# Placing norm, key and value pieces among the steps of the mixers, and the early banks of the merges, in a one-core hybrid decoder layer

## The chip, the core and the metric

The kernel runs on one core of a Trainium2 chip. A core has five engines with queues of their own: TensorE (PE in the profile: matmuls, with weight loads as PEld), VectorE (DVE), ScalarE (ACT), GpSimd (POOL) and SyncE (SP), the last of which only issues transfers here. The metric is the device time of one execution in microseconds; lower is better. The time before is 2633.38 us, the median of three runs (2632.34 to 2636.46).

## What is computed

One layer with 512 tokens of width 2048, in float32. The input is normalised and modulated to u, and one combined projection of u feeds three causal mixers in parallel:

```python
proj = jnp.einsum('bsd,de->bse', u, w_in)
o_a = diff_attention(a_q, a_k, a_v, lam, lam_init, da_norm_w)   # 8 heads, q and k in two maps of 64, v 128
o_b = retention(b_q, b_k, b_v, ret_norm_w)                      # 8 heads, rotated qk of 64, v 128
o_c = dilated_mixture(c_q, c_k, c_v)                            # 3 groups x 8 heads
y_a = jnp.einsum('bsw,wd->bsd', o_a * jax.nn.silu(a_z), w_proj_a)   # y_b and y_c likewise
merged = jax.nn.sigmoid(g_a) * y_a + jax.nn.sigmoid(g_b) * y_b + jax.nn.sigmoid(g_c) * y_c
y = jnp.einsum('bsd,de->bse', merged, w_out)
return x + gate[:, None] * y                                    # then one final RMSNorm
```

The outputs of differential attention and of retention are normalised per head (an RMS norm over the 128 channels of a head) and multiplied by silu of a gate column. That norm, the queries and keys of these two mixers, and the banks of the merges are what the change places anew.

## The kernel before

Every product is made of three matmuls, since each operand is held as a rounded high part and a low remainder: `mm3` issues high by high, high by low, low by high. Splitting an operand costs one ScalarE copy (the high part) and one VectorE subtraction (the low part), so behind each weight tile that TensorE reads stand one ACT `wh` and one DVE `wl`.

Behind the modulation (from L702) the instructions of the engines are pinned (L72), but for some transfers of POOL: each engine runs them in the order in which the program issues them. The order is thus written by hand, and an instruction that waits holds up all behind it on its engine.

**The step (L747).** The mixers and merges are cut into steps. `step()` issues the load of a later weight tile on SP (`feed`), the split of the tile that the second step from here will use (`cut`: `wh`, then `wl`), then every piece that lies in the list `late`, and hands out the tile that was split two steps ago. The caller then issues 24 matmuls with it (`half_mul`, L808: half of a projection of 128 columns). So the pieces of a step run on ACT and DVE beside the 24 matmuls of that step, and behind `wh` and `wl` of it. Weight tiles have three buffers each (`wr`, `wh`, `wl`).

**Banks.** The eight accumulator banks are two with the tag `pj` (projections) and six with the tag `at` (all else). A new tile takes a bank of its tag whose readers are done, and the matmul that writes it waits for them.

**Differential attention (L1367 to L1450)** takes one head at a time, in six steps `run(0)` to `run(5)`: queries' projection (0, 1), keys' (2, 3), gate column's (4, 5), then the scores of eight tiles (`a_scores`: each a DVE instruction `e<-at,cau` that adds the mask, and an exponential). `a_rest` is the list of what is left of a head, done in the six steps of the next one, as (piece within the step, piece after its matmuls): silu of the gate column; then the transposes; then the values; the squares for the norm, then their sum on PE; `gate`, which is `rms_gate` (ACT square root, DVE reciprocal of 128x512, two products); `put` (`yh`, `yl`, the split of the result for the merge). Beside them the loop places `query` in step 2, `keys` in step 4, two pieces `part` that sum a modulation row (steps 1 and 2), `values_split` (even heads, step 4) and, in heads 3 and 7, `gate_split` (step 5). `keys` makes four copies and two subtractions on a half of the partitions each, then two copies more.

**Retention (L1515 to L1591)** takes two heads at a time in eight steps: queries (0, 1), keys (2, 3), gate column of the first head (4, 5), scores of the first head, gate column of the second head (6), scores of the second head, (7), values of the first head. These four projections take turns on the two `pj` banks, so that the gate column of step 4 needs the bank of the queries and that of step 6 the bank of the keys. `rotate` reads a projection from its bank with four ACT copies (`rt`) and a DVE product (`rf<-pj,cos`). `query` runs in step 3, `keys` in step 4. `b_rest` has three entries, done in steps 0 to 2 of the next pair: silu and the squares of the first head, then on PE their sum and the values of the second head; squares of the second head, the whole norm of the first with its `put`, then a sum; the whole norm of the second head with its `put`.

**The merges (`gate_phase`, L832)** multiply the mixer's result by its output weights, 16 tiles of columns, each summed into a bank. The first six (four for the last merge, `AHEAD`, L767) begin before the mixer's last y tiles are there: `y_start` does the rows that exist, and the pieces `left` of the last head or pair are placed among these steps; `close` adds the missing rows and reads the bank with a DVE product. `close` of tiles 0 and 1 follows the seventh `y_start`, of 2 and 3 the eighth. Tiles 0 and 1 take `pj` banks, all others `at` banks (L841). Merge "first" follows the dilated windows, "mid" the attention, "last" the retention.

## Time and profile before

| stretch of the profiled execution | us | PE busy us | DVE busy us | ACT busy us | granted clock |
|---|---|---|---|---|---|
| first merge, 1611 to 1715 us | 104.0 | 102.5 | 41.7 | 36.2 | 1.00 |
| differential attention, 1715 to 2031 | 316.0 | 306.0 | 230.0 | 185.7 | 0.99 |
| mid merge, 2031 to 2128.5 | 97.5 | 92.5 | 55.2 | 29.4 | 0.98 |
| retention, 2128.5 to 2351 | 222.5 | 206.7 | 148.7 | 124.9 | 0.95 |
| last merge, 2351 to 2448 | 97.0 | 90.7 | 63.9 | 32.1 | 0.96 |
| whole span | 2634.7 | 2537.7 | 1924.4 | 1132.7 | 0.987 |

The profiled execution took 2636.43 us, 3.05 more than the median of the three timed runs, with 2634.7 us from its first to its last instruction. The busy times come from the profile's windows of each stretch, the last row from its page. A matmul of 512 columns is shown 0.39 us long, but the next one starts 0.23 us after it, since they are pipelined. The granted clock is the mean share of TensorE's full clock.

### The profile page before, as it was taken

The page shows a single profiled execution, that of the slowest core. Times are in us where ns is not written, and L with a number is a line of the kernel's source. Part 1 is how long each engine was busy: PE and PEld are TensorE (multiplying, and loading weights), DVE is VectorE, ACT ScalarE, POOL GpSimd, SP SyncE. Part 2 cuts the span into 40 slices and gives each one's busy share as a digit, 9 for nine tenths or more (in the row PEclk, how much of TensorE's full clock was granted, in tenths as well). Part 3 has the DMA queues.
Part 4 walks back from the last instruction along what each step waited for, and adds up shares of the span by engine and source line. Part 5 has one row for each costly group of instructions (what it writes and reads, how often), then busy time and mean ns, then how long its engine had stood idle before and what let it go on. Part 6 is the DMA issues. An engine that isn't in the chain of part 4 may idle for free. (4 is left out here: it accounts for less than half of the span.)

```text
span 2634.7 us, 36774 instructions
## 1 busy us (share of the span) xinstructions
PE 2537.7 (96%) x14539; PEld 2234.8 (85%) x14539; DVE 1924.4 (73%) x2682; ACT 1132.7 (43%) x1476; POOL 262.2 (10%) x327
## 2 busy tenths in 40 slices
PE   6999999999999999999999999999998999989998
PEld 5777877999999999998888888887787887777888
DVE  7994888778887787878786775367777557676654
ACT  4223433433443333333346665346656245553223
POOL 2342000000000000000000001200000210003200
PEclk9999999999999999999999999999999999999999
DMA  9776766666766666666665554653342663338643
GB/s 343 257 273 221 270 212 208 216 208 208 233 229 224 219 220 223 231 226 227 223 203 159 154 153 136 205 151 108 109 120 73 211 191 98 99 109 255 209 134 117
DMA packets 363953, 504.83 MB, mean 192 GB/s; under 512 B 18850, under 2 KB 237748, under 8 KB 363396
## 3 DMA queue, kind: packets, MB, share of 16 engines
q1 hardware_dynamic: 329732, 401.89, 47.7%
q0 software_dynamic: 27136, 92.13, 10.3%
q10 hardware_dynamic: 6912, 8.46, 0.9%
q8 instruction: 114, 1.87, 0.3%
q14 instruction: 59, 0.48, 0.1%
HBM read 450.37 MB, written 52.04 MB: 191 GB/s over the span
## 5 line engine op out<-in xcount | busy, mean ns | idle before, releaser
L86 ACT CAST xh<-xr 128x2048 fp32r<-128x2048 f32 x196 | 374.1, 1909 | 590.8 <-PE at L86 470.6
L86 DVE TENSOR_TENSOR xl<-xr,xh 128x2048 fp32r<-128x2048 f32 x196 | 449.1, 2291 | 187.3 <-ACT xh L86 186.2
L86 PE MATMUL pj<-uh,wh 128*128 128x512 f32 x944 | 376.2, 399 | 15.8 <-DVE rf L86 15.8
L86 DVE TENSOR_TENSOR wl<-wr,wh 128x1024 fp32r<-128x1024 f32 (+2 forms) x241 | 238.1, 1007 | 205.1 <-ACT wh L86 200.0
L86 PE MATMUL pj<-uh,wl 128*128 128x512 f32 x944 | 372.0, 394 | 2.6 <-POOL wl L172 2.6
L86 PE MATMUL pj<-ul,wh 128*128 128x512 f32 x944 | 372.1, 394 | 0.0
L86 ACT CAST wh<-wr 128x1024 fp32r<-128x1024 f32 (+2 forms) x275 | 239.1, 889 | 294.8 <-PE at L86 158.4
L86 DVE TENSOR_TENSOR xr<-xr 128x512 f32<-128x512 f32 x448 | 309.2, 690 | 16.0 <-DMA xr<-in_w_in_dram 4.6
L86 PE MATMUL at<-fh,xl 128*128 128x256 f32 x864 | 244.9, 283 | 2.1 <-DVE xl L86 2.1
L86 PE MATMUL at<-fh,xh 128*128 128x256 f32 x864 | 244.5, 283 | 0.0
L86 PE MATMUL at<-fl,xh 128*128 128x256 f32 x864 | 244.4, 283 | 0.0
L86 PEld LDWEIGHTS pj<-uh,wh 128*128 128x128 f32 x944 | 180.3, 191 | 53.2 <-DVE rf L86 17.0
L86 PEld LDWEIGHTS pj<-uh,wl 128*128 128x128 f32 x944 | 179.6, 190 | 41.6 <-POOL wl L172 3.0
L86 PEld LDWEIGHTS pj<-ul,wh 128*128 128x128 f32 x944 | 180.3, 191 | 36.3
L86 PEld LDWEIGHTS at<-fh,xl 128*128 128x128 f32 x864 | 165.8, 192 | 2.5 <-DVE xl L86 2.5
L86 PEld LDWEIGHTS at<-fh,xh 128*128 128x128 f32 x864 | 165.8, 192 | 0.0
L86 PEld LDWEIGHTS at<-fl,xh 128*128 128x128 f32 x864 | 165.8, 192 | 0.0
L86 PE MATMUL at<-uh,xh 128*128 128x256 f32 x576 | 163.0, 283 | 0.0
L86 PE MATMUL at<-ul,xh 128*128 128x256 f32 x576 | 163.0, 283 | 0.0
L86 PE MATMUL at<-uh,xl 128*128 128x256 f32 x576 | 163.0, 283 | 0.0
L86 PE MATMUL at<-yh,wh 128*128 128x512 f32 x336 | 132.2, 394 | 9.3 <-ACT wh L86 6.2
L86 PE MATMUL at<-yh,wl 128*128 128x512 f32 x336 | 131.7, 392 | 0.0
(387 smaller groups left out, 5702.2 us busy)
## 6 DMA issues: line engine op xcount, KB each, us to landing
xr<-in_w_in_dram SPq DMA_DIRECT2D x224, 512.0 KB, 4.6
xr<-in_w_in_dram SPq DMA_DIRECT2D x84, 1024.0 KB, 5.0
wr<-in_w_in_dram SPq DMA_DIRECT2D x116, 512.0 KB, 4.0
wa<-in_w_ada_dram SPq DMA_DIRECT2D x20, 1024.0 KB, 9.5
wr<-in_w_out_dram SPq DMA_DIRECT2D x32, 512.0 KB, 3.9
wr<-in_w_in_dram SPq DMA_DIRECT2D x32, 448.0 KB, 8.7
wb<-in_w_ada_dram SPq DMA_DIRECT2D x12, 1024.0 KB
bw<-in_w_in_dram SPq DMA_DIRECT2D x24, 384.0 KB, 5.5
```

The source lines that it names most:

```text
L86: return lambda *a, **k: pin(f(*a, **k))
```

## The change

Four things are moved; no arithmetic is added or taken away.

1. `rms_gate` is cut in two: `rms_root` (the square root on ACT) and `rms_gate` (reciprocal and two products on DVE).
2. Attention: in step 4 the order is square root, `keys`, then the rest of the norm; `keys` makes its last four copies in another order. The two `part` pieces go one step later (2 and 3), and `values_split` goes from step 4 of an even head to step 1 of the odd head behind it.
3. Retention: `query` goes from step 3 to step 2; in each step the pair's own piece goes ahead of what is left of the pair before. What is left is spread over steps 0 to 4: the first head's norm in step 1, its `put` in step 2, the second head's norm in step 3, its `put` in step 4. In the last pair the values of the first head go ahead of step 7, its squares into step 7, and the values of the second head ahead of the last merge.
4. Merges: tile 0, the last early tile (5, or 3 in the last merge) and tiles 10 and 15 take the `pj` banks, all others `at`.

```diff
@@ -838,7 +838,7 @@
 
         def y_start(db, nj):
             h, l = step()
-            py = pj() if db < 2 else at()
+            py = pj() if db in (0, n_ahead - 1, 10, 15) else at()
             for j in range(nj):
                 mm3(py, h[:, j, :], l[:, j, :], yh[j], yl[j], j == 0, j == 7)
             ahead[db] = py
@@ -861,8 +861,8 @@
 
         for db in range(n_ahead):
             before, after = left.pop(0) if left else (None, None)
-            if before is not None:
-                late.append(before)
+            if before:
+                late.extend(before if isinstance(before, tuple) else (before,))
             y_start(db, 8 - lacking)
             if after is not None:
                 after()
@@ -1241,13 +1241,15 @@
         dve.tensor_sub(sqs[64:P, :], sq[0], sqs[0:64, :].bitcast(F32))
         return sqs
 
-    def rms_gate(pool, o, ps, wcol, sz):
+    def rms_root(pool, ps):
         rs = pool.tile([P, S], F32, tag="rs", name="rs", bufs=1)
         act.activation(out=rs, in_=ps, func=AF.Sqrt, scale=1.0 / P, bias=eps)
+        return rs
+
+    def rms_gate(rs, o, wcol, sz):
         dve.reciprocal(rs, rs)
         dve.scalar_tensor_tensor(out=rs, in0=o, scalar=wcol, in1=rs, op0=ALU.mult, op1=ALU.mult)
         dve.tensor_mul(rs, rs, sz)
-        return rs
 
     a_es, ap = open_pool("ap", "left")
     cau = ap.tile([P, 512], F32, tag="cau", name="cau")
@@ -1383,13 +1385,16 @@
         def total():
             got["ps"] = rms_sum(got["sqs"])
 
+        def root():
+            got["rs"] = rms_root(ap, got["ps"])
+
         def gate():
-            got["y"] = rms_gate(ap, got["o"], got["ps"], daw, got["sz"])
+            rms_gate(got["rs"], got["o"], daw, got["sz"])
 
         def put():
-            put_y(ap, hd, got["y"])
-
-        return [(first, None), (None, turn), (None, values), (squares, total), (gate, None), (put, None)]
+            put_y(ap, hd, got["rs"])
+
+        return [((first,), None), ((), turn), ((), values), ((squares,), total), ((root, gate), None), ((put,), None)]
 
     def query(ps, qs):
         for m in range(2):
@@ -1408,16 +1413,17 @@
             dve.tensor_sub(kl[own, :], ps[own, :], kh[own, :].bitcast(F32))
         for (kh, kl), (own, other) in zip(ks_, sides):
             act.copy(kh[other, :], kh[own, :].bitcast(F32))
+        for (kh, kl), (own, other) in zip(ks_, sides):
             act.copy(kl[other, :], kl[own, :].bitcast(F32))
 
-    rest, chunk = [(None, None)] * 6, {}
+    rest, chunk = [((), None)] * 6, {}
     gate_load(0)
     gate_load(1)
     for hd in range(8):
         def run(i, ps, *pieces):
 
             before, after = rest[i]
-            late.extend(f for f in (before,) + pieces if f is not None)
+            late.extend(before[:1] + tuple(f for f in pieces if f is not None) + before[1:])
             half_mul(ps, i % 2, step())
             if after is not None:
                 after()
@@ -1431,16 +1437,16 @@
         n, last_part = hd // 4, hd % 4 == 3
         ps = pj()
         run(0, ps)
-        run(1, ps, lambda: part(0))
+        run(1, ps, (lambda: values_split(*v)) if hd % 2 else None)
         qs = [ap.tile([P, S], F32R, tag=f"q{m}", name=f"q{m}") for m in range(2)]
         qps, ps = ps, pj()
-        run(2, ps, lambda: query(qps, qs), lambda: part(1))
+        run(2, ps, lambda: query(qps, qs), lambda: part(0))
         if hd % 2 == 0:
             v = values_of(ap, 0, hd * P)
-        run(3, ps)
+        run(3, ps, lambda: part(1))
         ks_ = [tuple(ap.tile([P, S], F32R, tag=f"k{m}{x}", name=f"k{m}{x}") for x in "hl") for m in range(2)]
         kps, ps = ps, pj()
-        run(4, ps, lambda: keys(kps, ks_), (lambda: values_split(*v)) if hd % 2 == 0 else None)
+        run(4, ps, lambda: keys(kps, ks_))
         run(5, ps, (lambda: chunk.update(parts=gate_split(n))) if last_part else None)
         es, sts = [], []
         a_scores(qs, ks_, es, sts)
@@ -1513,32 +1519,44 @@
 
 
     def b_rest(pr, ps, got, values):
-        def first():
-            got["sz"].append(silu(bp, ps, tag="sz1", bufs=1))
-            got["sqs"] = rms_squares(bp, got[0], "0")
-
-        def total():
-            got["ps"] = rms_sum(got["sqs"])
-
-        def second():
-            total()
+        def squares(a):
+            got["s", a] = rms_squares(bp, got[a], str(a))
+
+        def total(a):
+            got["p", a] = rms_sum(got["s", a])
+
+        def root(a):
+            got["r", a] = rms_root(bp, got["p", a])
+
+        def gate(a):
+            rms_gate(got["r", a], got[a], ret_col, got["z", a])
+
+        def put(a):
+            put_y(bp, 2 * pr + a, got["r", a])
+
+        def z():
+            got["z", 1] = silu(bp, ps, tag="sz1", bufs=1)
+
+        def value():
             got[1] = values(1)
 
-        def between():
-            sqs = rms_squares(bp, got[1], "1")
-            put_y(bp, 2 * pr, rms_gate(bp, got[0], got["ps"], ret_col, got["sz"][0]))
-            got["sqs"] = sqs
-
-        def last():
-            put_y(bp, 2 * pr + 1, rms_gate(bp, got[1], got["ps"], ret_col, got["sz"][1]))
-
-        return [(first, second), (between, total), (last, None)]
-
-    rest = [(None, None)] * 3
+        def both(*fs):
+            return lambda: [f() for f in fs]
+
+        if pr < 3:
+            return [((z, lambda: squares(0)), both(lambda: total(0), value)),
+                    ((lambda: squares(1), lambda: root(0), lambda: gate(0)), lambda: total(1)),
+                    ((lambda: put(0),), None), ((lambda: root(1), lambda: gate(1)), None),
+                    ((lambda: put(1),), None)]
+        return [both(lambda: squares(0)), both(value, lambda: total(0)),
+                (both(z, lambda: squares(1), lambda: root(0), lambda: gate(0)), lambda: total(1)),
+                (both(lambda: put(0), lambda: root(1), lambda: gate(1)), None), (lambda: put(1), None)]
+
+    rest = [((), None)] * 5
     for pr in range(4):
         def run(i, ps, *pieces):
-            before, after = rest[i] if i < 3 else (None, None)
-            late.extend(f for f in (before,) + pieces if f is not None)
+            before, after = rest[i] if i < 5 else ((), None)
+            late.extend(pieces + before)
             half_mul(ps, i % 2, step())
             if after is not None:
                 after()
@@ -1571,24 +1589,30 @@
         run(1, qps)
         decs = [decay(2 * pr + a) for a in range(2)]
         kps = pj()
-        run(2, kps)
+        run(2, kps, lambda: query(qps))
         v = values_of(bp, 1, 2 * pr * P)
-        run(3, kps, lambda: query(qps))
+        run(3, kps)
         zps = pj()
         run(4, zps, lambda: keys(kps))
         run(5, zps, lambda: values_split(*v))
-        pts, got = ([], []), {"sz": []}
+        pts, got = ([], []), {}
         b_scores(2 * pr, ks_[0], qs[0], pts[0], decs[0])
         ps = pj()
-        run(6, ps, lambda: got["sz"].append(silu(bp, zps, tag="sz0", bufs=1)))
+        run(6, ps, lambda: got.update({("z", 0): silu(bp, zps, tag="sz0", bufs=1)}))
         b_scores(2 * pr + 1, ks_[1], qs[1], pts[1], decs[1])
-        run(7, ps)
 
         def values(a, pr=pr, v=v, pts=pts):
             return b_values(2 * pr + a, *v, pts[a])
 
-        got[0] = values(0)
         rest = b_rest(pr, ps, got, values)
+        if pr < 3:
+            run(7, ps)
+            got[0] = values(0)
+        else:
+            got[0] = values(0)
+            run(7, ps, rest[0])
+            rest[1]()
+            rest = rest[2:]
     m_es, mh, ml = None, [], []
 
     def merged_open():
```

## The prediction

> **What bounds the kernel now.** First the page, for the engine that is the bound; then the waits of that engine over the whole span, of which these belong to the stages that the change touches; then the windows of the stretches at half clock behind them.

> ```profile
> PE 2537.7 (96%) x14539; PEld 2234.8 (85%) x14539; DVE 1924.4 (73%) x2682; ACT 1132.7 (43%) x1476; POOL 262.2 (10%) x327
> ...
> PE pj L86 <- DVE rf L86: 15.8, 3, 5.3
> PE at L86 <- DVE st L86: 10.0, 7, 1.9
> ...
> PE at L86 <- ACT wh L86: 6.2, 1, 6.2
> ...
> PE pj L86 <- DVE sz L86: 3.5, 1, 3.5
> ...
> PE at L86 <- DVE gpr L86: 1.5, 1, 1.5
> PE at L86 <- DVE q L86: 1.5, 1, 1.5
> ```

> The columns are total us, times, longest. TensorE is the bound: only time in which it stands still can be won, and no matmul is removed. `rf` is retention's step 4, which waits for the bank that `query` must read (pairs 1 to 3); `st` the last score tiles of attention heads 1 to 7, which wait for a bank that the first score reduction frees; `wh` the last merge's fifth tile, the first that needs all of y; `sz` the mid merge's tile 1, waiting for a `pj` bank; `gpr` and `q` tile 8 of the first and mid merges, waiting for the bank of tile 2. Together 38.5 us.

> ```profile
> 1825.10:1828.50 3.40, 3.40 (x10) 2.63 (x9) 3.29 (x15) 3.40 (x13) 0.00 (x0) 0.50 0.45 136
> ...
> 2376.00:2381.50 5.50, 5.44 (x12) 3.85 (x13) 2.36 (x2) 0.92 (x1) 0.00 (x0) 0.50 0.52 141
> sum 28.70, PE 28.64 PEld 22.11 DVE 19.07 ACT 16.66 POOL 2.73; mean PE 4.09 PEld 3.16 DVE 2.72 ACT 2.38 POOL 0.39
> 1907.00:1910.40 3.40, 2.97 (x13) 2.48 (x14) 3.37 (x18) 2.99 (x13) 0.00 (x0) 1.00 0.55 159
> ```

> These are the first and last of seven such stretches and their sum (28.7 us); the third number from the right is the granted clock. Each stands right behind a wait: two in attention (3.4 us each), one behind `sz` (3.4), one behind each `rf` (4.4, 4.3, 4.3), one behind `wh` (5.5). At half clock half of the time is lost, some 14 us more. The last row shows that a wait of 1.9 us doesn't always bring it.

> **Attention.** The end of head 2, VectorE, then ScalarE, then TensorE:

> ```profile
> 1812.76 3.35 DVE L86 RECIPROCAL rs<-rs 128x512 f32<-128x512 f32 x1 [0.78 <-ACT rs L86]
> ...
> 1817.55 0.68 DVE L86 TENSOR_TENSOR k0l<-pj,k0h 64x512 fp32r<-64x512 f32 x1
> ...
> 1822.28 1.22 DVE L86 TENSOR_TENSOR wl<-wr,wh 128x1024 fp32r<-128x1024 f32 x1
> 1823.42 0.69 DVE L86 TENSOR_TENSOR yl<-rs,yh 128x512 fp32r<-128x512 f32 x1
> 1824.13 0.29 DVE L86 CUSTOM_DVE_ANT_0 e<-at,cau 128x128 f32<-128x128 f32 x1
> ...
> 1813.22 0.58 ACT L86 CAST k1h<-pj 64x512 fp32r<-64x512 f32 x1
> ...
> 1820.58 0.39 PE L86 MATMUL pj<-uh,wl 128*128 128x512 f32 x1
> 1820.80 0.22 PE L86 MATMUL at<-k0h,q 128*128 128x128 f32 x1
> ...
> 1822.25 0.34 PE L86 MATMUL at<-k1l,q 128*128 128x384 f32 x1
> 1824.48 0.50 PE L86 MATMUL at<-k0h,q 128*128 128x512 f32 x1 [1.90 <-DVE st L86]
> ```

> The seventh score tile is due about 0.17 us behind 1822.25, at 1822.4, but the first reduction comes at 1824.13, as keys and `values_split` stand behind the norm. In the new order the keys' subtractions start when the copy of 1813.22 is done, at 1813.8, and end two times 0.7 later, at 1815.2. Then come reciprocal and products (1812.76 to 1817.55, so 4.8), at 1820.0 step 5's `wl` (1822.28 to 1823.42, 1.15), `yl` (0.7), and at 1821.85 the first reduction, which frees its bank by 1822.1: 0.3 us ahead of need. Heads 3 and 7 have `gate_split` before it, one more subtraction of 0.7, and stay 0.4 us short. The parts (two DVE products) and `values_split` now lie in steps 1 to 3, where DVE has idle time before its next `wl`; they cost TensorE nothing as long as the transposes' splits aren't held up. Each `part` also issues a load on POOL's queue for the part two on, needed a head later (some 38 us), so a step's delay is hidden; SP's loads keep their places. Each wait costs 0.16 us more than shown, since matmuls 0.39 long start 0.22 apart. Gain: 10.0 + 7 x 0.16 + half of 6.8, less 0.8 for heads 3 and 7: **13.7 us**.

> **Merges.** Tile 1 of the mid merge now takes an `at` bank: at that time the score banks have been read, so `sz` goes (3.5, and half of 3.4). The bank of tile 1, not 2, is what tile 8 needs; `close` of tile 1 comes one `y_start` sooner (24 matmuls at 0.22, over 5 us, against waits of 1.5). `at` must hold tiles 1 to 4, the values and the norm's sum: six, just enough. Gain: 3.5 + 1.7 + 1.5 + 1.5 + 3 x 0.16: **8.7 us**. If one bank more were held, tile 4 would wait until the norm's product has read the values: some 2.0 from table load to reciprocal (2359.86 to 2361.87, below), then 4.2 (3.4 and 0.8), and half a clock stretch of 1.7: the lower bound is 0.8 us.

> **Retention, pairs 1 and 2.** From the first norm's reciprocal to the first score product of pair 1, with VectorE's waits between:

> ```profile
> 2189.13 3.35 DVE L86 RECIPROCAL rs<-rs 128x512 f32<-128x512 f32 x1 [1.32 <-ACT rs L86]
> ...
> 2212.42 0.69 DVE L86 TENSOR_TENSOR rf<-pj,cos 128x512 f32<-128x512 f32 x1 [1.15 <-ACT rt L86]
> ...
> 2221.69 0.68 DVE L86 TENSOR_TENSOR pf<-at,dec 128x512 f32<-128x512 f32 x1
> ...
> DVE wl L86 <- PE pj L86: 2.3, 1, 2.3
> DVE rf L86 <- ACT rt L86: 2.3, 2, 1.1
> DVE yl L86 <- ACT yh L86: 1.4, 2, 0.7
> ...
> DVE wl L86 <- ACT wh L86: 0.8, 3, 0.3
> ...
> 2206.38 0.80 PE L86 MATMUL pj<-uh,wh 128*128 128x512 f32 x1 [5.25 <-DVE rf L86]
> ...
> 2217.04 0.62 ACT L86 CAST k0l<-k0l 64x512 fp32r<-64x512 f32 x1
> ...
> 2238.70 0.69 DVE L86 TENSOR_TENSOR sqs<-sq,sqs 64x512 fp32r<-64x512 f32 x1 [0.69 <-ACT sqs L86]
> ...
> 2240.29 0.40 PE L86 MATMUL at<-sqs,ones_r 128*128 128x512 f32 x1
> ```

> With `query` in step 2, behind only one norm, DVE reads the queries' bank about 2195.1 to 2195.8 (reciprocal and products 4.8 behind 2189.13, then a `wl`); step 4 needs it at 2201.0 (2206.38 less its wait, with the 0.16). The `rf` wait goes: 15.8 / 3 + 0.16 + 2.2 for the half clock, 7.6 us a pair. But this time was also slack for ACT and DVE, which carry a chain through the whole pair. DVE's work in it stays; its four kinds of waits above (6.8 us) shrink to some 2.3, since ACT makes `rt` and `yh` while DVE does a norm, and starts that now abut win 0.4. So `pf` comes 4.9 us sooner, TensorE 7.6. Two new waits follow. The scores need the low keys: `cos` moves from 2212.42 to 2207.05, so that the ACT copy `k0l` (2217.04 + 0.62) ends at 2212.3; halves 4 and 5 (48 matmuls, 10.9) end at 2211.9 and the second score matmul is due 0.2 later: **0.2 late**. The norm's sum of the next pair: `sqs` was done at 2239.4, 0.9 ahead of 2240.29; with 7.6 - 0.2 - 4.9 = 2.5 less, TensorE waits **1.6**. Gain: 2 x (7.6 - 1.8) = **11.6 us**.

> **Pair 3 and the last merge.** Here the same chain runs on into the merge. VectorE, then ScalarE:

> ```profile
> 2337.77 1.15 DVE L86 TENSOR_TENSOR pf<-at,dec 128x512 f32<-128x512 f32 x2
> ...
> 2345.05 1.15 DVE L86 TENSOR_TENSOR pf<-at,gpr 128x512 f32<-128x512 f32 x2
> ...
> 2361.87 3.35 DVE L86 RECIPROCAL rs<-rs 128x512 f32<-128x512 f32 x1 [1.32 <-ACT rs L86]
> ...
> 2376.00 2.36 DVE L86 TENSOR_TENSOR wl<-wr,wh 128x1024 fp32r<-128x1024 f32 x2 [0.26 <-ACT wh L86]
> ...
> 2348.74 2.00 ACT L86 CAST wh<-wr 128x1024 fp32r<-128x1024 f32 x2
> ...
> 2351.13 0.58 ACT L86 ACTIVATE sq<-at 64x512 f32<-64x512 f32 x1
> ...
> 2357.27 0.59 ACT L86 ACTIVATE sq<-at 64x512 f32<-64x512 f32 x1 [1.21 <-PE at L86]
> ...
> 2359.86 1.28 ACT L86 ACT_TABLE_LOAD   x1
> ```

> From `pf` of the first head to `pf` of the second it is 7.3 us, to step 7's `wh` 3.7 more, and so it stays. The new order then has on ACT: that `wh` (1.0), the squares of head 0 (2357.27 to 2359.86, 2.6), another `wh` and a silu (1.4: two `wh` and a silu lie between 2348.74 and 2351.13), and from the squares of head 1 to the reciprocal 4.7 (2357.27 to 2361.87 is 4.6). Sum 20.7 behind `pf`; before it was 24.1, as the squares of head 1 had to wait for values that TensorE made only behind a merge tile. From the reciprocal to tile 4's `wl` it is 14.1 with the same pieces as before: `put` and the norm of head 1, its `put`, and two `wl`. So tile 4, the first that needs all of y, is ready 4.9 + 3.4 and thus 8.3 us sooner, measured from a step 4 that didn't wait.

> TensorE would be there before. From step 4 it has four halves (5.5 each), two scores (1.2 each and the 0.2), two values (1.9 each), two sums (0.2 each) and four early tiles of 18 matmuls (4.1 each), 45.2 in all; the chain has 2221.69 - 2201.0 - 4.9 = 15.8 to `pf`, then 20.7 + 14.1 and the 1.2 of `wl`, 51.8. So TensorE waits some 6.6 in two places: 2.7 at the sum behind step 7 (`sqs` of head 0 is done 7.3 + 3.7 + 4.2 behind `pf`, so at 31.0, while the values end at 28.3), the rest at tile 4. The chain doesn't pass through the four early tiles, so the first wait only makes the second one shorter. I take the half clock to come again at tile 4 (1.7 lost, before it was 2.1). Gain: 8.3 + 0.4, **8.7 us**.

> **Sum.** 13.7 + 8.7 + 11.6 + 8.7 = 42.7. The profiled execution would go from 2636.4 to 2593.7; it stood 3.05 above the median shown, so I forecast 2633.4 - 42.7 = **2590.7**. Each term is bounded: from above by the waits and half-clock losses it takes away (attention 14.5, merges 8.7, retention and last merge 3 x 7.6 + 6.4 + 2.1 = 31.3), so 54.5 in all. The lower bounds are the 0.8 of the merges and what rivals (a) and (b) leave of retention and attention.

> On the clock, the row of 1825.10 stands behind a wait of 1.9 us, that of 1907.00 behind an equal one at full clock. [...]

> **Rivals.** (a) *The chain of ACT and DVE is longer than my ledger*: every us that it misses is paid in pairs 1, 2 and 3, and waits of 2 us and more also halve the clock. For: four waits that I say vanish rest on ACT being early, and everything in these steps is one chain of two engines. Against: every duration in it is a row of this trace. With 2 us more a pair and two more half clocks (1.7 each): 2590.7 + 6 + 3.4 = 2600. (b) *Attention's reductions stay late*, since the reciprocal now stands between keys and scores: the margin is 0.3 us. If 1 us is missing in each of seven heads, with one half clock: 2590.7 + 8 = 2598.7. (c) *The order isn't what holds the banks*, as when the bank that a wait names is freed by something else than the moved piece: the waits stay, 2628 to 2634. Against: each wait's releaser is the DVE instruction behind the moved piece. (d) *Slower: the clock stays at half behind the new, shorter waits*. Place: behind the sums of retention. Half rate loses 0.5 us a us, so it takes 97 us at half clock to lose the 43 and 5.3 besides: 2639 and more. Against: the seven stretches end within 3.4 to 5.5 us of work. [...]

> **Chances.** My forecast, 2584 to 2596: 0.66. (a) 0.17, (b) 0.08, better than forecast 0.04, (c) 0.03, (d) 0.02. 0.2% is 5.3 us, about what a measurement of this kernel tells from no change: faster 0.95, same 0.03, slower 0.02. The range takes in (a) and (b): 2583 to 2603.

> **What would show it.** TensorE's waits for `rf`, `sz`, `gpr` and `q` gone, for `st` under 1.5 us in total; in their place waits for `sqs` of 1 to 2 us in two pairs and near 3 in the last, 0.2 for `k0l`, and for `wh` about 2.5 at the fifth tile; half clock left in at most three places of these stages. Wrong: `st` above 4, any wait at step 4 of retention, or a merge tile waiting for a bank, which the six `at` banks would show.

## The result, and the profile after

The changed kernel took 2592.86 us (median of four runs, 2589.22 to 2595.30) beside 2633.89 us of the kernel before; the ratio is 0.9842 (0.9825 to 0.9859). In a later set of runs it took 2590.89 us (five runs, 2588.81 to 2591.55) against 2633.98 (nine runs, 2630.36 to 2637.97). The forecast was 2590.7.

First the busy line of the page of after:

```profile
PE 2519.2 (97%) x14539; PEld 2222.9 (86%) x14539; DVE 1924.0 (74%) x2682; ACT 1134.5 (44%) x1476; POOL 263.7 (10%) x327
```

Then TensorE's waits over the whole span, of which these stand in the touched stages (total us, times, longest):

```profile
PE at L86 <- DVE sqs L86: 5.3, 3, 2.5
...
PE at L86 <- ACT wh L86: 2.1, 1, 2.1
PE at L86 <- DVE wl L86: 0.5, 1, 0.5
...
PE at L86 <- DVE st L86: 0.3, 2, 0.2
```

`rf`, `sz`, `gpr` and `q` are gone, `st` is down from seven waits to two, `wh` from 6.2 to 2.1, and `sqs` and a short wait for `wl` have come in. The same 14539 matmuls take 18.5 us less of PE's busy time (2537.7 before). Of that, some 14.3 are, by the granted clock of 0.50, half of the 28.64 us that it was busy at half clock in these stages. That is an estimate: in before a matmul of 512 columns starts 0.43 us behind the one ahead of it at half clock (1825.87 to 1826.30) and 0.23 at full clock, which would make it 13.3. VectorE and ScalarE do the same work as before. The windows of the touched stages, with the granted clock third from the right:

```profile
1611.00:1715.00 104.00, 104.00 (x487) 87.06 (x487) 42.88 (x64) 37.24 (x55) 20.90 (x37) 1.00 0.60 187
1715.00:2029.00 314.00, 313.68 (x1484) 263.01 (x1483) 242.10 (x458) 196.09 (x348) 14.73 (x23) 1.00 0.40 117
2029.00:2120.00 91.00, 91.00 (x407) 75.52 (x406) 48.55 (x68) 25.57 (x39) 26.09 (x49) 1.00 0.80 251
2120.00:2305.00 185.00, 181.96 (x841) 151.45 (x840) 136.82 (x206) 114.72 (x200) 4.31 (x8) 1.00 0.35 100
2305.00:2410.00 105.00, 99.79 (x442) 82.08 (x441) 72.68 (x89) 38.91 (x52) 29.88 (x56) 1.00 0.74 239
```

In the first three TensorE is busy all the time but for 0.3 us (second number against first). What is left stands in retention (3.0 us) and in pair 3's end with the last merge (5.2), all at full clock.

TensorE issues 14539 matmuls in every version, so the versions can be compared stage by stage, by the time between the same two matmuls by their place in the order. The table does so for the kernels of this study; its borders are the matmuls that start at 1611, 1715, 2029, 2120, 2305 and 2480 us in after. The wait of the mid merge's tile 1 falls into the second column.

| us | first merge | attention, first mid tiles | mid merge | retention | pair 3's end, last merge and beyond | sum |
|---|---|---|---|---|---|---|
| before | 105.87 | 333.64 | 92.81 | 204.37 | 177.30 | 913.99 |
| after | 104.10 | 314.03 | 91.05 | 184.96 | 174.83 | 868.97 |
| after, second set | 104.10 | 314.07 | 91.05 | 184.94 | 174.85 | 869.01 |
| e1, attention alone | 105.89 | 319.44 | 92.84 | 204.53 | 177.32 | 900.02 |
| e2, merges alone | 104.10 | 329.79 | 91.05 | 203.64 | 177.27 | 905.85 |
| e3, retention alone | 105.89 | 333.69 | 92.84 | 184.86 | 174.81 | 892.09 |
| e4 | 104.10 | 314.02 | 91.05 | 191.00 | 174.81 | 874.98 |
| e5 | 104.10 | 327.88 | 91.05 | 184.96 | 174.83 | 882.82 |
| e6 | 104.10 | 321.56 | 91.05 | 185.24 | 174.84 | 876.79 |
| e7 | 104.10 | 314.03 | 91.05 | 199.91 | 178.29 | 887.38 |
| e8 | 104.10 | 314.01 | 91.05 | 180.98 | 172.37 | 862.51 |

The touched stages became 45.0 us shorter. Two executions of the changed kernel agree in them within 0.04 us. The time ahead of them, from the first matmul on, was 1600.1 to 1606.9 us in the twelve profiled executions: most of what makes one run differ from the next lies outside of the change.

### The profile page after: what moved, and what is told of

It is laid out like the page before. It is cut to its first block, busy times and chain, and to the rows that moved or that the text cites. A ratio compares the mean times of both kernels' runs of the same rounds, so it can differ in the third digit from the quotient of the medians.

```text
span 2590.2 us, 36747 instructions
## 1 busy us (share of the span) xinstructions
PE 2519.2 (97%) x14539; PEld 2222.9 (86%) x14539; DVE 1924.0 (74%) x2682; ACT 1134.5 (44%) x1476; POOL 263.7 (10%) x327
## 5 line engine op out<-in xcount | busy, mean ns | idle before, releaser
L86 ACT CAST xh<-xr 128x2048 fp32r<-128x2048 f32 x196 | 374.4, 1910 | 589.1 <-PE at L86 471.0
L86 DVE TENSOR_TENSOR xl<-xr,xh 128x2048 fp32r<-128x2048 f32 x196 | 449.1, 2291 | 184.5 <-ACT xh L86 183.3
L86 PE MATMUL pj<-uh,wh 128*128 128x512 f32 x944 | 372.5, 395 | 0.0
L86 PE MATMUL pj<-uh,wl 128*128 128x512 f32 x944 | 369.4, 391 | 2.6 <-POOL wl L172 2.6
L86 PE MATMUL pj<-ul,wh 128*128 128x512 f32 x944 | 369.1, 391 | 0.0
L86 DVE TENSOR_TENSOR wl<-wr,wh 128x1024 fp32r<-128x1024 f32 (+2 forms) x241 | 238.2, 1007 | 174.8 <-ACT wh L86 173.8
L86 ACT CAST wh<-wr 128x1024 fp32r<-128x1024 f32 (+2 forms) x275 | 239.1, 889 | 285.5 <-PE at L86 136.2
L86 DVE TENSOR_TENSOR xr<-xr 128x512 f32<-128x512 f32 x448 | 309.2, 690 | 15.0 <-DMA xr<-in_w_in_dram 3.3
L86 PE MATMUL at<-fh,xl 128*128 128x256 f32 x864 | 245.0, 284 | 1.9 <-DVE xl L86 1.9
L86 PE MATMUL at<-fh,xh 128*128 128x256 f32 x864 | 244.5, 283 | 0.0
L86 PE MATMUL at<-fl,xh 128*128 128x256 f32 x864 | 244.5, 283 | 0.0
L86 PEld LDWEIGHTS pj<-uh,wl 128*128 128x128 f32 x944 | 178.0, 189 | 40.8 <-POOL wl L172 3.0
L86 PEld LDWEIGHTS pj<-uh,wh 128*128 128x128 f32 x944 | 178.4, 189 | 35.6
L86 PEld LDWEIGHTS pj<-ul,wh 128*128 128x128 f32 x944 | 178.2, 189 | 35.6
L86 PEld LDWEIGHTS at<-fh,xl 128*128 128x128 f32 x864 | 165.5, 192 | 2.3 <-DVE xl L86 2.3
L86 PEld LDWEIGHTS at<-fh,xh 128*128 128x128 f32 x864 | 165.5, 192 | 0.0
L86 PEld LDWEIGHTS at<-fl,xh 128*128 128x128 f32 x864 | 165.5, 192 | 0.0
L86 PE MATMUL at<-ul,xh 128*128 128x256 f32 x576 | 163.0, 283 | 0.0
L86 PE MATMUL at<-uh,xh 128*128 128x256 f32 x576 | 163.0, 283 | 0.0
L86 PE MATMUL at<-uh,xl 128*128 128x256 f32 x576 | 163.0, 283 | 0.0
L86 PE MATMUL at<-yh,wh 128*128 128x512 f32 x288 | 112.5, 390 | 2.1 <-ACT wh L86 2.1
L86 PE MATMUL at<-yh,wl 128*128 128x512 f32 x288 | 112.2, 390 | 0.5 <-DVE wl L86 0.5
```

Source lines behind the costliest of these rows:

```text
L86: return lambda *a, **k: pin(f(*a, **k))
```

## The experiments

Times are medians; "before" stands for the runs of the kernel before on the same chip (2634.50 for e1 to e4, 2633.95 for e5 to e8, 2633.98 for the last two).

### The three parts by themselves: e1, e2, e3

Each is the kernel before with one part of the change: e1 has the attention hunks alone, e2 the one line on the banks, e3 the retention hunks with the last merge's pieces.

> The attention part alone, merges and retention as before. Theory (the three parts act on separate waits and add up): 13.7 us faster than before, so about 2620; the waits for st fall from 10.0 us to under 0.5, while rf (15.8), wh (6.2), sz (3.5), gpr and q (1.5 each) stay. Rival (the score tiles wait because banks are scarce, not because VectorE is late): st stays near 10 us and the time near 2634.

```diff
-        run(4, ps, lambda: keys(kps, ks_), (lambda: values_split(*v)) if hd % 2 == 0 else None)
+        run(4, ps, lambda: keys(kps, ks_))
...
-            late.extend(f for f in (before,) + pieces if f is not None)
+            late.extend(before[:1] + tuple(f for f in pieces if f is not None) + before[1:])
```

> The bank choice of the merges alone. Theory: 8.7 us faster than before, about 2625; the waits for sz, gpr and q go, those for rf, st and wh stay as before. Rival (VectorE is late anyway, so another tile waits in the place of tile 1 or 8, or tile 4 for its sixth bank): a new wait of 2 to 6 us in the mid merge and at most 3 us gained, about 2631.

```diff
-            py = pj() if db < 2 else at()
+            py = pj() if db in (0, n_ahead - 1, 10, 15) else at()
```

> The retention part alone (with the last pair's), attention and merges as before. Theory: 20.3 us faster than before, about 2613.6; rf and the 6.2 us for wh go, in their place sqs 1.5, 1.5 and 2.7 us and about 2.5 us at the last merge's fifth tile; st, sz, gpr and q stay. Rival (the last pair's gain rests on tile 3's pj bank): without it a tile of the last merge waits for a bank by 3 us and more, and under 17 us are gained, above 2617.

```diff
-        run(2, kps)
+        run(2, kps, lambda: query(qps))
...
-        return [(first, second), (between, total), (last, None)]
...
+        if pr < 3:
+            return [((z, lambda: squares(0)), both(lambda: total(0), value)),
+                    ((lambda: squares(1), lambda: root(0), lambda: gate(0)), lambda: total(1)),
...
```

| | us | ratio to before | waits of TensorE left in the touched stages |
|---|---|---|---|
| e1 | 2621.83 | 0.9952 (0.9938 to 0.9965) | rf 15.8, wh 6.2, sz 3.5, gpr 1.5, q 1.5, st 0.3 |
| e2 | 2625.22 | 0.9964 (0.9951 to 0.9976) | rf 15.8, st 10.0, wh 6.2 |
| e3 | 2613.01 | 0.9918 (0.9904 to 0.9931) | st 10.0, sqs 5.3, sz 3.5, gpr 1.5, q 1.5, wh 0.7, wl 0.5 |

Against before they won 12.7, 9.3 and 21.5 us, 43.4 in all, where the whole change won 41.0 and, in the second set, 43.1. By the sums of the table it is 14.0, 8.1 and 21.9, 44.0 against 45.0. So the parts hardly help or hinder one another. Each took away its own waits and no others, and the three rivals fell. By the stages, attention won 333.64 - 319.44 = 14.2. The merges won 1.77 + 1.76 in two columns and, between e1 and after, 319.44 - 314.03 = 5.4 in the second: 8.9. Retention with what follows won 19.5 + 2.5 = 22.0 in e3. In e2 the second column shows only 3.9, where 5.4 lie between e1 and after. By an estimate that no view here shows, one more stretch at half clock stood behind attention's waits in that execution than the two of before (1825.08 and 1988.92), 1.7 us; with these 1.7 the three parts would stand at 45.7, 0.7 above the whole.

### The place of the query: e4 and e7

e4 is the changed kernel with the query one step later. e7 has it early, but with the norms placed as before.

> The changed kernel with the queries' piece back in retention's step 3, ahead of the second norm. Theory (what holds the bank is the number of norms in front of the queries, so one norm is early enough; the step decides how late the keys come): no wait for rf at step 4, but the keys' chain comes some 2.2 us later, so the scores of pairs 1 to 3 wait about 2.4 us for k0l in place of 0.2; about 6.6 us slower than the changed kernel, near 2599.5, more by up to 5 where the clock is halved. Rival (the earlier step is what frees the bank): rf waits of about 5 us come back in pairs 1 to 3, near 2615.

```diff
-        run(2, kps, lambda: query(qps))
+        run(2, kps)
...
-        run(3, kps)
+        run(3, kps, lambda: query(qps))
```

It took 2597.89 us, 0.986 (0.9847 to 0.9874) of before. TensorE's waits in e4, whole span, and then two matmuls of pair 1 with the wait before them:

```profile
PE at L86 <- DVE sqs L86: 5.2, 3, 2.5
...
PE at L86 <- ACT k0l L86: 4.3, 3, 1.4
...
PE at L86 <- ACT k0h L86: 1.1, 3, 0.4
```

```profile
2191.05 0.50 PE L86 MATMUL at<-q,k0h 128*128 128x512 f32 x1 [0.37 <-ACT k0h L86]
...
2192.97 0.51 PE L86 MATMUL at<-q,k0l 128*128 128x512 f32 x1 [1.42 <-ACT k0l L86]
```

No wait for `rf` came back: with one norm less ahead of it, the query is in time even in step 3. But the keys' copies end later, and the scores wait for them. The retention column grew by 6.0, 2.0 a pair. So the early step is worth 2.0 a pair because it lets the keys go earlier, not because of the bank.

> The changed kernel, but retention's norms in their old three entries, the first of which is split over steps 0 to 2 of the next pair as before, with only query moved to step 2 ahead of the norm that stands there. Theory (one norm per step is what makes room; moving the queries ahead only passes the lateness on to the keys): no wait for rf, but the keys' copies end late and the scores wait near 5 us in each of pairs 1 to 3, with the clock at half behind some of them; the last merge waits near 6 us for wh as before. Time 2609 to 2612. Rival (the bank that query frees is all of it): no such wait at the scores, 2597 or less.

```diff
-        if pr < 3:
-            return [((z, lambda: squares(0)), both(lambda: total(0), value)),
-                    ((lambda: squares(1), lambda: root(0), lambda: gate(0)), lambda: total(1)),
...
+        return [(first, second), (between, total), (last, None)]
```

It took 2608.69 us, 0.9903 (0.9889 to 0.9918). The waits in e7, whole span:

```profile
PE pj L86 <- ACT wh L86: 6.3, 3, 2.1
PE at L86 <- ACT wh L86: 6.2, 1, 6.2
...
PE at L86 <- ACT k0l L86: 2.5, 3, 1.4
```

The size is as the theory had it, the place is not. Most of the lateness shows as a wait for step 5's weights. ScalarE in pair 1, start, duration and, in brackets, its idle time:

```profile
2175.23 0.69 ACT L86 ACTIVATE rs<-at,eps 128x512 f32<-128x512 f32 x1
2180.93 0.62 ACT L86 CAST yh<-rs 128x512 fp32r<-128x512 f32 x1 [5.01 <-DVE rs L86]
2181.45 1.99 ACT L86 CAST wh<-wr 128x1024 fp32r<-128x1024 f32 x2
```

`put` stands in the same entry as its norm. So ScalarE comes to `yh` at once behind the square root, stands 5.0 us until VectorE has done the norm, and the two weight splits behind `yh` are late with it. In the changed kernel `put` is a step later, and those splits are not behind it. With half clock behind these waits (in pair 1 the matmuls start 0.43 us apart up to 2186.79, then 0.23) the retention column is 15.0 us longer than in after, 5.0 a pair, and the last merge has its wait of 6.2 back.

### Attention: e5 and e6

e5 keeps the keys ahead of the norm and puts the other pieces back; e6 does the opposite.

> The changed kernel, but attention's other pieces stand where they stood before: the products of the gate in steps 1 and 2 behind the query, values_split of even heads in step 4 behind the keys; the keys still stand ahead of the rest of the norm. Theory (the norm's chain sets the first score reduction, so both moves are needed): in the heads 2, 4 and 6 the three subtractions of values_split now stand between keys and reciprocal, so the seventh score tile waits 2.6 to 2.8 us in each of them; the odd heads wait no more than in the changed kernel (0.3). Waits for st near 8 us in all, time 2601 to 2606. Rival (the keys' place alone does it): waits for st below 1 us in all and the time of the changed kernel, 2593.

```diff
-        run(1, ps, (lambda: values_split(*v)) if hd % 2 else None)
+        run(1, ps, lambda: part(0))
...
-        run(2, ps, lambda: query(qps, qs), lambda: part(0))
+        run(2, ps, lambda: query(qps, qs), lambda: part(1))
...
-        run(3, ps, lambda: part(1))
+        run(3, ps)
...
-        run(4, ps, lambda: keys(kps, ks_))
+        run(4, ps, lambda: keys(kps, ks_), (lambda: values_split(*v)) if hd % 2 == 0 else None)
```

It took 2605.05 us, 0.9893 (0.9878 to 0.9908). VectorE at the end of head 2 in e5:

```profile
1815.72 0.70 DVE L86 TENSOR_TENSOR k1l<-pj,k1h 64x512 fp32r<-64x512 f32 x1
1818.54 1.23 DVE L86 TENSOR_TENSOR vl<-vl,vh 128x1024 fp32r<-128x1024 f32 x1 [2.12 <-ACT vh L86]
1819.68 3.35 DVE L86 RECIPROCAL rs<-rs 128x512 f32<-128x512 f32 x1
```

The subtraction of `values_split` takes 1.2 us, but VectorE stands 2.1 before it, since its `vh` lies on ScalarE behind the keys' copies; the reciprocal comes 3.3 us behind the keys, where in after it follows them at once. TensorE waits for `st` 6.3 us in five heads, longest 2.0, and for the norm's products (`rs`) 1.7 in three. Behind the longest, ahead of 1826.55, the matmuls start 0.43 us apart in place of 0.23: half clock. Together the second column grew by 13.9. The waits are 7.7 of that more than in after, and 0.16 for each of six more makes 1.0; the other 5.2 are, by estimate, three stretches at half clock of 1.7 each.

> The changed kernel, but in attention the whole norm (root, reciprocal, products) again stands ahead of the keys in step 4, and the copies of keys go in their old order; the products of the gate and values_split are at their new places. Theory: the reciprocal then holds up the keys' subtractions, their copies hold ScalarE at step 5's wh, and every head waits as the odd heads did before: five times 0.8 us and twice 1.4 us for st, 6.6 us in all, time near 2600.5. Rival (the places of values_split and of the gate's products were all of it): waits for st of 0.3 us as in the changed kernel, 2593.

```diff
-        return [((first,), None), ((), turn), ((), values), ((squares,), total), ((root, gate), None), ((put,), None)]
+        return [((first,), None), ((), turn), ((), values), ((squares,), total), ((lambda: [root(), gate()],), None), ((put,), None)]
...
-        for (kh, kl), (own, other) in zip(ks_, sides):
             act.copy(kl[other, :], kl[own, :].bitcast(F32))
```

It took 2599.79 us, 0.9869 (0.9852 to 0.9885), with `st` at 6.6 in seven heads, longest 1.4, to the tenth what the theory gave. ScalarE at the end of head 2:

```profile
1813.87 0.61 ACT L86 CAST k0h<-k0h 64x512 fp32r<-64x512 f32 x1
1818.42 0.62 ACT L86 CAST k0l<-k0l 64x512 fp32r<-64x512 f32 x1 [3.94 <-DVE k0l L86]
...
1820.22 1.05 ACT L86 CAST wh<-wr 128x1024 fp32r<-128x1024 f32 x1
```

The copy of `k0l` waits 3.9 us for a subtraction that stands behind the reciprocal, and step 5's `wh` behind it. Both moves of the change are needed, e5 for the even heads and e6 for all.

### The sums later: e8, and e9 with e10 beside it

> A try at a faster version: the changed kernel, but the second head's values stand ahead of the first head's sum in pairs 0 to 2; in the last pair that sum stands behind the first early tile, and the norm's pieces one early tile later. Theory (these waits are only a matter of where the sum is put): the waits for sqs in pairs 1 and 2 (1.5 us each) go, that of the last pair (2.7) goes too, and the fifth tile is waited for as long or a little longer: 5.4 us gained at most, 2587.5. Rival (the chain of ScalarE and VectorE takes it back at the third or fourth tile of the merge and at the scores of the next pair): 3 us or less gained, 2590 or more.

```diff
-            return [((z, lambda: squares(0)), both(lambda: total(0), value)),
+            return [((z, lambda: squares(0)), both(value, lambda: total(0))),
...
-        return [both(lambda: squares(0)), both(value, lambda: total(0)),
-                (both(z, lambda: squares(1), lambda: root(0), lambda: gate(0)), lambda: total(1)),
-                (both(lambda: put(0), lambda: root(1), lambda: gate(1)), None), (lambda: put(1), None)]
+        return [both(lambda: squares(0)), value,
+                (both(z, lambda: squares(1)), lambda: total(0)),
+                (both(lambda: root(0), lambda: gate(0)), lambda: total(1)),
+                (both(lambda: put(0), lambda: root(1)), None),
+                (lambda: gate(1), lambda: late.append(lambda: put(1)))]
```

It took 2584.05 us, 0.9811 (0.9796 to 0.9825). Since the changed kernel had run on another chip, both ran once more together:

> The changed kernel itself, on the same chip and beside the same runs of the kernel before as the next one, so that the two can be compared without the difference between chips (the changed kernel and e8_sums_later were measured on two chips, at 2592.9 and 2584.1). Expected 2592.9, within 2 us.

> The kernel of e8_sums_later once more, beside the changed kernel on one chip. By the traces, the waits of the touched stages are 6.5 us less than in the changed kernel (9.6 against 3.1); the rest of the 8.8 us between the two medians lies in stages that neither touches and should not come again. Theory: 6 to 7 us faster than the changed kernel of this call. Rival (the two chips differ, and the waits come back elsewhere): 3 us or less.

e9 took 2590.89 us, 0.9834 (0.9821 to 0.9847) of before, 2.0 under what was expected of it, and e10 2584.14, 0.981 (0.9796 to 0.9823): 6.75 us faster than the changed kernel, as the stages say (869.01 - 862.58 = 6.4, with 862.58 for e10's five columns). The theory of e8 had 5.4 at most, its rival 3. All of TensorE's waits in retention and the last merge of e10, matmul by matmul:

```profile
2322.39 0.50 PE L86 MATMUL at<-yh,wh 128*128 128x512 f32 x1 [0.47 <-ACT wh L86]
...
2323.65 0.50 PE L86 MATMUL at<-yh,wl 128*128 128x512 f32 x1 [0.53 <-DVE wl L86]
...
2329.07 0.50 PE L86 MATMUL at<-yh,wh 128*128 128x512 f32 x1 [0.82 <-ACT yh L86]
...
2330.16 0.50 PE L86 MATMUL at<-yl,wh 128*128 128x512 f32 x1 [0.58 <-DVE yl L86]
```

Tile 4 and its last three matmuls wait about as long as tile 4 did. But the three waits for `sqs` are gone, and so are the three for the low keys, which the theory had not counted on. What shortened the chain is seen on ScalarE behind the values of pair 1's first head, in after:

```profile
2208.45 0.57 ACT L86 ACTIVATE sq<-at 64x512 f32<-64x512 f32 x1
...
2214.19 0.59 ACT L86 ACTIVATE sq<-at 64x512 f32<-64x512 f32 x1 [1.88 <-PE at L86]
...
2218.07 0.69 ACT L86 ACTIVATE rs<-at,eps 128x512 f32<-128x512 f32 x1
```

and in e10:

```profile
2205.48 0.61 ACT L86 ACTIVATE sq<-at 64x512 f32<-64x512 f32 x1
...
2209.40 0.59 ACT L86 ACTIVATE sq<-at 64x512 f32<-64x512 f32 x1
...
2213.28 0.69 ACT L86 ACTIVATE rs<-at,eps 128x512 f32<-128x512 f32 x1
```

In after the engines wait for each other in a ring: TensorE holds the second head's values back while it waits for the squares' sum, and ScalarE then waits 1.9 us for those values. With the values ahead of the sum it is 7.8 us instead of 9.6 from the first square to the root. The kernel of e8 and e10 is the fastest of this study.

## Why the prediction was right

**Attention** (13.7 forecast, 14.2 measured). The ledger had the first reduction 0.55 us ahead of the seventh score tile (1821.85 against 1822.4). In after, at the end of head 2, first VectorE, then the seventh tile on TensorE:

```profile
1811.55 0.68 DVE L86 TENSOR_TENSOR k0l<-pj,k0h 64x512 fp32r<-64x512 f32 x1 [1.85 <-ACT k1h L86]
...
1812.99 3.35 DVE L86 RECIPROCAL rs<-rs 128x512 f32<-128x512 f32 x1
...
1818.91 0.69 DVE L86 TENSOR_TENSOR yl<-rs,yh 128x512 fp32r<-128x512 f32 x1
1819.51 0.28 DVE L86 CUSTOM_DVE_ANT_0 e<-at,cau 128x128 f32<-128x128 f32 x1
...
1820.14 0.39 PE L86 MATMUL at<-k0h,q 128*128 128x512 f32 x1
```

It is 1820.14 - 1819.51 = 0.63, and the tile doesn't wait. Heads 3 and 7 lose 0.32 each (forecast 0.4). Rival (b) fell, but it was near: e5 and e6 show that one move left out costs 13.9 and 7.5 us of this stage.

**Merges** (8.7 forecast, 8.9 measured). No tile of the merges waits for a bank, so the six `at` banks suffice.

**Retention, pairs 1 and 2.** The new waits came where they were put: in the trace's starts, 0.27 and 0.26 lost at the low keys (forecast 0.2), and twice 1.52 at the sum (1.6). Rival (a), a chain longer than the ledger, fell with that; e4 and e7 show what such lateness costs, 2.0 and 5.0 us a pair. Retention and last merge together were forecast at 11.6 + 8.7 = 20.3 and won 19.4 + 2.5 = 21.9.

**Pair 3 and the last merge** hold most of the difference. The first wait was forecast at 2.7 and lost 2.74. Behind it the prediction said: "I take the half clock to come again at tile 4 (1.7 lost, before it was 2.1)". This is the step that failed. Waits of TensorE there in after, and then in the second set of the same kernel (e9):

```profile
2314.26 0.50 PE L86 MATMUL at<-sqs,ones_r 128*128 128x512 f32 x1 [2.53 <-DVE sqs L86]
...
2333.51 0.50 PE L86 MATMUL at<-yh,wh 128*128 128x512 f32 x1 [2.14 <-ACT wh L86]
...
2334.78 0.50 PE L86 MATMUL at<-yh,wl 128*128 128x512 f32 x1 [0.54 <-DVE wl L86]
```

```profile
2312.57 0.50 PE L86 MATMUL at<-sqs,ones_r 128*128 128x512 f32 x1 [2.51 <-DVE sqs L86]
...
2331.81 0.50 PE L86 MATMUL at<-yh,wh 128*128 128x512 f32 x1 [0.49 <-ACT wh L86]
```

In after no stretch of the touched stages was at half clock. In e9 there was one, behind the sum (2313.96 to 2317.36, granted 0.50), and it cost nothing: the chain of ScalarE and VectorE sets the start of tile 4, so TensorE came there 1.65 us later and waited 1.65 less. Both executions need the same time for this stage, 174.83 and 174.85. So do e3, e4, e5 and e6, which have the same order here (174.81 to 174.84). In e3 and e4 half clock is seen behind the sum (e3: matmuls 0.43 us apart from 2336.89 on; e4: granted 0.50 from 2321.75 to 2325.16), and in all four tile 4 waits 0.5 to 0.7 us for `wh`, near the 0.5 of e9. None of the six is longer by the 1.7 that half clock behind tile 4 was to cost. Without these 1.7, the forecast for the touched stages would have been 44.4 of the 45.0 measured.

By the starts of the matmuls, pairs 1 and 2 won 11.4 us (forecast 11.6), and pair 3 with the last merge 10.5 (8.7). Tile 4 came 8.5 sooner, where the chain gave 8.3; the other 2.0, where the working had 0.4, lie behind it, where before lost 2.1 at half clock. The chain itself was right: the first matmul that reads tile 4's `wl` starts 51.7 behind the first of step 4 (2334.78 - 2283.08), and the ledger had 51.8. But the two waits with that for `wl` came to 5.75 (2.74, 2.30 and 0.71 lost), and the working had 6.6. It counted TensorE's work only up to tile 4's first matmul (45.2, measured 45.4), and `wl` is read by its third, two matmuls later. The 6.6 went into no gain, so this slip cost the forecast nothing.

**The sum** was 42.7; the profiled execution went from 2636.43 to 2591.96, by 44.5, the 45.0 of the stages less 0.5 in earlier ones. That the median came out 2.2 above the forecast and not below it has its reason in where the profiled executions stand: before's stood 2.5 above the median shown with the result, after's 0.9 below its own. So it is luck in part that 2590.7 lies so near to the medians of both sets: they moved by 41.0 and 43.1, and the stages that the working was about by 45.0.

**Rivals (c) and (d)** fell: e2 took exactly the merges' three waits for banks away, and the stretches worked at half clock in the touched stages went from 28.7 us to none.

**The clock.** In after the new waits left the clock whole, the longest of them 2.53 us. But e9 is the same kernel, and there half clock followed a wait of 2.51 us. So rival (a), which let waits of 2 us and more halve the clock, had it too simple: in before the five over 2 us of these stages were followed by half clock (3.5 to 6.2 us), in after those of 2.53 and 2.14 were not. The last section has the measured cases.

## What to carry to other kernels

Where engines run in an order written by hand, work out for each bank and each operand when it is due and what stands ahead of it on its engine; such a ledger was right to 0.1 us here for the waits at the sums, the keys and the scores, and for the end of the longest chain. What it had 0.9 too long was the wait there, since it counted to the tile's first matmul and not to the one that reads the operand. An instruction that must wait should stand behind all work that doesn't need it, on the waiting engine too: TensorE's sum ahead of independent values cost 2.0 us a pair (after against e10), and the old order of the norms, with ScalarE's `yh` in the same entry as its norm, 5.0 (e7). Half clock on TensorE cost nothing here where another engine's chain set the next start (e9's last column, 174.85, against 174.83 in after).

## What the runs showed of the hardware

```profile
2329.90:2333.30 3.40, 1.47 (x7) 0.89 (x5) 3.33 (x5) 1.41 (x2) 0.00 (x0) 1.00 0.00 0
2333.31:2336.72 3.41, 2.67 (x10) 1.91 (x11) 2.55 (x3) 1.10 (x2) 0.00 (x0) 1.00 0.62 172
```

```profile
2310.55:2313.95 3.40, 1.39 (x6) 1.17 (x7) 2.46 (x4) 2.74 (x5) 0.00 (x0) 1.00 1.00 378
2313.96:2317.36 3.40, 3.40 (x10) 2.63 (x9) 1.91 (x4) 2.59 (x4) 0.54 (x1) 0.50 0.83 246
```

```profile
1821.66:1825.07 3.41, 1.51 (x9) 1.10 (x9) 3.38 (x10) 2.80 (x6) 0.00 (x0) 1.00 0.07 17
1903.58:1906.99 3.41, 1.95 (x14) 1.58 (x12) 2.91 (x3) 3.23 (x4) 0.00 (x0) 1.00 0.00 0
1906.99:1910.40 3.41, 2.97 (x13) 2.48 (x14) 3.38 (x18) 2.99 (x13) 0.00 (x0) 1.00 0.55 159
```

In after TensorE stands still for 1.93 us of the first stretch and keeps its clock; in e9 it stands for 2.01, and the clock is halved; in before it stands for 1.90 up to 1825.07, and the clock is halved as well. The lengths of matmuls in the profile overlap (0.39 us long, 0.23 apart), and with these lengths no border can be read off: 1.90 us came with half clock and 1.93 without. What the cases show is that a wait of 2.53 us that is split between two such stretches (the sum's in after, 1.08 ahead of 2312.81 and 1.45 behind it) cost nothing more, and that one of 1.90 that lies within one was followed by half clock (before, at 1825). The two equal waits of before that the prediction could not tell apart fit this: the one ahead of 1824.48 lay in one stretch, of the one ahead of 1907.43 0.44 us lay in the next, with 1.46 ahead of it. That the place is the cause is an estimate from these cases; no run moved a wait and nothing else.
